# The expert loop of a mixture-of-experts stage: ScalarE's order written out by hand, and other PSUM banks for the last expert's products

## The chip, the cores and the metric

The kernel runs on one core of one Trainium2 chip. The metric is the device time of one execution in microseconds; lower is better. The core has a TensorE (PE) for matrix products and transposes, a VectorE (DVE), a ScalarE (ACT), a GpSimd (POOL), and a SyncE (SP) that here issues the loads. PE writes its products into PSUM, which this stage divides into eight banks of 512 fp32 numbers per partition; everything else lives in SBUF.

## The reference, cut to what matters

The program computes two transformer blocks in a row on 1024 positions of width 1024, in fp32. The change touches only the mixture of experts that ends block one: 32 experts of inner width 512, two per token.

```python
D_MODEL = 1024; SEQ = 1024; N_EXPERTS = 32; TOP_K = 2; D_EXPERT = 512
def hier_moe(xn, w_route_group, b_route_group, w_route_expert, b_route_expert, w_gate, w_up, w_down):
...
    def expert_block(args):
        xblk, e = args
        hdn = jax.nn.silu(xblk @ w_gate[e]) * (xblk @ w_up[e])
        return hdn @ w_down[e]
...
def first_block(...):
...
        h = h + mixed @ w_out[l]
        h = h + hier_moe(rms_norm(h, norm2_gain[l]), ...)
    return rms_norm(h, final_norm_gain)
```

`second_block` (attention, two convolution mixers and a feed-forward part) follows on that result.

## The kernel before, in words

**One expert.** Each expert has 96 slots for tokens. Its six weight tiles of 1 MB (`mw`: two of gate, two of up, two of down) are loaded on SP's queue into a ring of 17 buffers (L996), so that a load is issued when the tile 17 places ahead of it has been used. An fp32 product is made of three fast ones (`mm3`, L38 to L40): each operand is split into a rounded part (`hi`, a ScalarE copy) and the rest (`lo`, a VectorE subtraction that follows it), and PE adds hi times lo, lo times hi and hi times hi. `split` (L1158 on ScalarE, L1163 on VectorE) does it for half a weight tile at a time, into a ring of four pairs `mhi`, `mlo`. An expert e goes through:

- `gather`: GpSimd fetches the 96 rows of its tokens into `xg`;
- `xT`: PE turns them round with eight transposes into PSUM (`mtr`, L1173), ScalarE evicts them as `xhi` (two instructions, L1176) and as `xf` (L1179), VectorE makes `xlo`;
- `up`: four chunks each of gate (`pg`) and up (`pu`): eight splits, 42 fast matmuls and two in plain fp32 (from `xf`, L1192, each drawn as two), then `silu` on ScalarE (`hd<-pg`, L1198) and the multiply with `pu` on VectorE (`hd<-hd,pu`, L1199);
- `down`: four transposes of `hd` (L1205), the split of the result (`hhi`, L1210; `hlo`, L1211), and 24 matmuls over four chunks of down's weights into `py`; then ScalarE copies `py` to SBUF (`ye<-py`, L1223) and GpSimd scatters it to memory (L1224). For the last expert VectorE copies one half (L1220) and ScalarE the other (L1221), and its `hhi` and `hlo` lie in buffers named `xhi` and `xlo`.

**PSUM.** `pg`, `pu` and `mtr` have two buffers of one bank each. `py` has a single buffer of two banks, so that all eight banks are taken: the next expert's first product into `py` has to wait until `ye<-py` has read it.

**Order.** The program writes up(e), xT(e+1), gather(e+2), down(e-1) for each e, and a scheduler puts the instructions of each engine's queue in order, by its own estimates and by a few priorities (`high_priority` on silu, the multiply, and the eviction of `hd`'s transposes). Engines take their queues in the order so fixed, which is the same in every execution. Behind the last expert come loads of the scattered rows, a sum and a normalization, and then block two; while the last expert runs, ScalarE and VectorE already split some weights of block two (`wthi`, `wtlo`, L1393 and L1394).

Of the kernel before, what the change touches and what calls it, by code (L numbers as in the profile page):

```python
# [12 lines left out]
F32 = mybir.dt.float32  # L13
F32R = mybir.dt.float32r
# [6 lines left out]
P = 128  # L21
# [998 lines left out]
def moe(tc, K, a, xn, lg, w12, yd, wst, s_m, then):  # L1020
# [119 lines left out]

    ps = xctx.enter_context(tc.tile_pool(name="mps", bufs=2, space=PSUM))

    def expert(xg, idx_g, idx_s, get, nye, last=False, behind=None):

        st = {}

        def gather():
            return nc.gpsimd.indirect_dma_start(out=xg, out_offset=None, in_=xn,  # L1148
                                                in_offset=bass.IndirectOffsetOnAxis(ap=idx_g, axis=0),
                                                bounds_check=S - 1, oob_is_err=False)  # L1150

        def split(w, c):
            if c % 2 == 0:
                st[w] = get()
            n = 512 if w != "d" and c == 3 else 1024
            src = st[w][:, (c % 2) * 1024:(c % 2) * 1024 + n]
            hi, lo = (t[:, 0:n] for t in spl.tiles([([P, 1024], "mhi"), ([P, 1024], "mlo")], F32R, len(spl.slots)))
            nc.scalar.activation(hi, src, AF.Copy)  # L1158
            with ExitStack() as held:
                if behind:  # L1160
                    held.enter_context(tc.issue_after(behind.ins))
# [4 lines left out]
        def xT():  # L1166
            hi = act.tile([P, 7, SLOTS], F32R, name="xhi")
            lo = act.tile([P, 7, SLOTS], F32R, name="xlo")
            xf = act.tile([P, SLOTS], F32, name="xf")
            for q in range(2):  # L1170
                p = ps.tile([P, 4, SLOTS], F32, name="mtr")
                for k in range(4):
                    nc.tensor.transpose(p[:, k, :], xg[:, 4 * q + k::8], K.ident[:SLOTS, :SLOTS])  # L1173
                n = 4 - q
                h = hi[:, 4 * q:4 * q + n, :]
                nc.scalar.activation(h, p[:, 0:n], AF.Copy)  # L1176
                V.tensor_sub(lo[:, 4 * q:4 * q + n, :], p[:, 0:n], h.bitcast(F32))  # L1177
                if q:
                    nc.scalar.activation(xf, p[:, 3], AF.Copy)  # L1179
            st["x"] = hi, lo, xf  # L1180

        def up():
            pg = ps.tile([SLOTS, 512], F32, name="pg")
            pu = ps.tile([SLOTS, 512], F32, name="pu")
            xhi, xlo, xf = st["x"]
            for c in range(4):
                for w, o in (("g", pg), ("u", pu)):
                    hi, lo = split(w, c)
                    for j in range(2):
                        k = 2 * c + j  # L1190
                        if k == 7:
                            nc.tensor.matmul(o, xf, st[w][:, 1536:2048], start=False, stop=True)  # L1192
                            continue
                        mm3(nc, o, xhi[:, k, :], xlo[:, k, :], hi[:, j * 512:(j + 1) * 512],
                            lo[:, j * 512:(j + 1) * 512], k == 0, False)
            hd = act.tile([SLOTS, 512], F32, name="hd", bufs=1)
            with tc.high_priority(offset=MPRI):
                nc.scalar.activation(hd, pg, AF.Silu)  # L1198
                V.tensor_mul(hd, hd, pu)  # L1199
            st["h"] = hd  # L1200

        def down():
            p = ps.tile([P, 4, SLOTS], F32, name="mtr")
            for k in range(4):
                nc.tensor.transpose(p[:, k, :], st["h"][:, k::4], K.ident[:SLOTS, :SLOTS])  # L1205

            hhi, hlo = (act.tile([P, 7, SLOTS], F32R, name="x" + n)[:, 0:4] if last else
                        act.tile([P, 4, SLOTS], F32R, name="h" + n, bufs=1) for n in ("hi", "lo"))
            with tc.high_priority(offset=MPRI):
                nc.scalar.activation(hhi, p, AF.Copy)  # L1210
                V.tensor_sub(hlo, p, hhi.bitcast(F32))  # L1211
            py = ps.tile([SLOTS, 1024], F32, name="py", bufs=1)
            for k in range(4):
                hi, lo = split("d", k)
                for c in range(2):
                    mm3(nc, py[:, c * 512:(c + 1) * 512], hhi[:, k, :], hlo[:, k, :],
                        hi[:, c * 512:(c + 1) * 512], lo[:, c * 512:(c + 1) * 512], k == 0, k == 3)
            y = act.tile([SLOTS, D], F32, name="ye", bufs=nye)
            if last:
                V.tensor_copy(y[:, 0:512], py[:, 0:512])  # L1220
                nc.scalar.activation(y[:, 512:], py[:, 512:], AF.Copy)  # L1221
            else:
                nc.scalar.activation(y, py, AF.Copy)  # L1223
            return nc.gpsimd.indirect_dma_start(  # L1224
                out=yd, out_offset=bass.IndirectOffsetOnAxis(ap=idx_s, axis=0), in_=y, in_offset=None,
                bounds_check=2 * S - 1, oob_is_err=False)

        return gather, xT, up, down
# [5 lines left out]
    E = [expert(xgs[e % NX], gidx[:SLOTS, e:e + 1], sidx[:SLOTS, e:e + 1], wst.get, 2, e + 1 == NE, None if e else known)  # L1234
         for e in range(NE)]
    scat = []
    for e in range(NX):
        g = E[e][0]()
# [23 lines left out]
    with tc.If(over > 0):  # L1262
# [23 lines left out]
        with tc.For_i(0, NE, 1) as e:  # L1286
            n = nc.values_load(nb[0:1, bass.ds(e, 1)], min_val=0, max_val=MORE + 1)
            with tc.For_i(1, n, 1) as b:
                V.tensor_copy(si, sof[:, bass.ds(e * MORE + b - 1, 1)])
                V.tensor_copy(gi, gof[:, bass.ds(e * MORE + b - 1, 1)])  # L1290

                def dyn(w, i):
                    return [P, 2048], lambda t: nc.sync.dma_start(
                        t, a[WN[w]][bass.ds(e, 1), :, i * 2048:(i + 1) * 2048].rearrange("o p f -> (o p) f"))
                ws = Stream(raw, [dyn(w, i) for w2 in ("gu", "d") for i in range(2) for w in w2], 5, "mw")
                for f in expert(xg, gi[:SLOTS], si[:SLOTS], ws.get, 1):
                    f()
        ctx.close()


# [1067 lines left out]
```

## Time and profile before

| | us |
|---|---|
| median of 3 runs (lowest to highest) | 2686.21 (2682.15 to 2687.73) |
| the profiled execution, its own time | 2681.36 |
| its span, first to last instruction | 2679.6 |
| first multiply `hd<-hd,pu` (expert 0) to the last (expert 31), starts | 831.24 to 1421.69 |

The rows shown further down are of the one profiled execution. Times count from the first instruction; "x2" at a row's end means two instructions drawn together; an idle time in brackets lies ahead of the instruction, with what ended it behind the arrow. The granted clock (PEclk) is PE's clock as a share of full speed, 1.00 being 2.4 GHz. The multiply L1199 occurs once per expert and so serves as a milestone: the stretch between two of them is one expert's turn.

### The profile page before, as it was taken

What the parts mean: (1) busy time and instruction counts of PE and PEld (TensorE: products, weight loads), DVE (VectorE), ACT (ScalarE), POOL (GpSimd) and SP (SyncE); (2) the same over time, 40 slices, a digit from 0 to 9 for tenths busy, and PEclk for the clock granted to TensorE, in tenths of its full rate; (3) what the DMA queues carried; (4) which work ended last, traced back from release to release, by engine and by line L of the source; (5) the groups of instructions that cost most, each with busy time, mean ns of one, the idle gap of its engine ahead of it and who ended that gap; (6) DMA issues with size and microseconds to landing.
All of it is one profiled execution on the core that took longest, in us unless ns stands there. A gap on an engine that the chain in (4) does not pass through costs nothing.

```text
span 2679.6 us, 42090 instructions
## 1 busy us (share of the span) xinstructions
PE 2519.2 (94%) x15498; PEld 1961.9 (73%) x15499; DVE 1872.9 (70%) x3258; ACT 1385.2 (52%) x2503; POOL 615.6 (23%) x1144
## 2 busy tenths in 40 slices
PE   7999999998988999999995999999999999999998
PEld 5777777776776676666664888777787788888786
DVE  5565767677347878877776664677558898777757
ACT  6443444444226777767675432456545445455444
POOL 1344566665212111111102212212010110000001
PEclk9999999998998999999997999999999999999999
DMA  5533112113478999989866211002124663224935
GB/s 185 168 111 101 51 38 66 29 45 140 158 282 300 371 382 366 362 334 347 331 237 232 86 48 32 24 1 62 58 81 136 225 215 119 83 79 148 341 121 181
DMA packets 170820, 447.11 MB, mean 167 GB/s; under 512 B 42928, under 2 KB 82224, under 8 KB 146032
## 3 DMA queue, kind: packets, MB, share of 16 engines
q1 hardware_dynamic: 150848, 381.17, 40.4%
q0 software_dynamic: 19760, 63.20, 6.5%
q8 instruction: 124, 2.03, 0.3%
q14 instruction: 88, 0.72, 0.1%
HBM read 382.43 MB, written 70.25 MB: 169 GB/s over the span
## 4 chain that ended last, share of the span: by engine, by line
PE 57%; issue 23%; DVE 8%; POOL 6%; DMA 3%; ACT 2%; SPq 0%; POOLq 0%; DVEq 0%; ACTq 0%
PE pa L1993 8%; PE pj L38 6%; PE pj L39 6%; PE pj L40 6%; PE pd L1993 4%; PE pe L1993 2%; PE po L38 2%; PE po L39 2%; PE po L40 2%; POOL xg L1148 2%; PE pe L2219 2%; PE O L1845 2%; PE px L2219 2%; PE T L1835 1%; POOL yd L1224 1%
## 5 line engine op out<-in xcount | busy, mean ns | idle before, releaser
L1163 DVE TENSOR_TENSOR mlo<-mw,mhi 128x1024 fp32r<-128x1024 f32 (+1 forms) x384 | 427.0, 1133 | 133.7 <-ACT mhi L1158 131.6
L1158 ACT ACTIVATE mhi<-mw 128x1024 fp32r<-128x1024 f32 (+1 forms) x384 | 375.6, 986 | 161.4 <-PE py L40 51.5
L38 PE MATMUL py<-mhi,hlo 128*96 128x512 f32 x248 | 106.1, 428 | 20.2 <-ACT ye L1223 15.1
L1224 POOL DMA_INDIRECT yd<-ye,sidx x32 | 35.3, 1103 | 360.6 <-ACT ye L1223 352.8
L2047 DVE SCALAR_TENSOR_TENSOR y<-c,pc,y 128x1023 f32<-128x1023 f32 x88 | 111.9, 1278 | 5.6 <-ACT y L2045 5.5
L38 PE MATMUL pj<-whi,xlo 128*128 128x512 f32 x256 | 106.3, 415 | 1.1 <-DVE gh L476 1.1
L39 PE MATMUL pj<-wlo,xhi 128*128 128x512 f32 x256 | 103.4, 404 | 0.0
L40 PE MATMUL pj<-whi,xhi 128*128 128x512 f32 x256 | 103.3, 403 | 0.0
L40 PE MATMUL py<-mhi,hhi 128*96 128x512 f32 x248 | 99.5, 401 | 0.0
L39 PE MATMUL py<-mlo,hhi 128*96 128x512 f32 x248 | 99.4, 401 | 0.0
L38 PE MATMUL pu<-mhi,xlo 128*96 128x512 f32 x224 | 96.6, 431 | 0.0
L38 PE MATMUL pj<-xhi,wclo 128*128 128x512 f32 x224 | 91.3, 407 | 4.2 <-ACT pj L1471 4.2
L39 PE MATMUL pu<-mlo,xhi 128*96 128x512 f32 x224 | 95.0, 424 | 0.0
L662 POOL TENSOR_TENSOR Xt<-Tm,Xi 128x15 f32<-128x15 f32 (+7 forms) x240 | 73.9, 308 | 76.3 <-DVE Tm L655 61.6
L38 PE MATMUL pj<-xhi,wlo 128*128 128x512 f32 x224 | 89.3, 403 | 1.9 <-ACT xhi L278 1.1
L39 PE MATMUL pj<-xlo,whi 128*128 128x512 f32 x224 | 90.5, 404 | 0.3 <-DVE xlo L279 0.3
L40 PE MATMUL pj<-xhi,wchi 128*128 128x512 f32 x224 | 90.5, 404 | 0.0
L38 PE MATMUL pg<-mhi,xlo 128*96 128x512 f32 x224 | 89.8, 401 | 0.5 <-DVE xlo L1177 0.5
L39 PE MATMUL pj<-xlo,wchi 128*128 128x512 f32 x224 | 90.3, 403 | 0.0
L40 PE MATMUL pj<-xhi,whi 128*128 128x512 f32 x224 | 90.2, 403 | 0.0
L1148 POOL DMA_INDIRECT xg<-xnd,gidx x32 | 44.5, 1390 | 195.3 <-PE mtr L1173 186.8
L39 PE MATMUL pg<-mlo,xhi 128*96 128x512 f32 x224 | 89.2, 398 | 0.0
(729 smaller groups left out, 7603.6 us busy)
## 6 DMA issues: line engine op xcount, KB each, us to landing
mw<-w_down SPq DMA_DIRECT2D x64, 1024.0 KB, 10.1
mw<-w_up SPq DMA_DIRECT2D x63, 1024.0 KB, 7.5
mw<-w_gate SPq DMA_DIRECT2D x62, 1024.0 KB, 9.5
wf<-ffn_up SPq DMA_DIRECT2D x44, 512.0 KB, 3.4
hr<-hdn SPq DMA_DIRECT2D x77, 256.0 KB, 5.0
w<-w_rwkv SPq DMA_DIRECT2D x28, 512.0 KB, 4.8
tq<-ffn_down SPq DMA_DIRECT2D x44, 256.0 KB, 3.6
td<-tq POOLq DMA_DIRECT2D x22, 512.0 KB, 3.6
```

Source lines behind the costliest of these rows:

```text
L38: nc.tensor.matmul(out, ll, rh, start=first, stop=False)
L39: nc.tensor.matmul(out, lh, rl, start=False, stop=False)
L40: return nc.tensor.matmul(out, lh, rh, start=False, stop=last)
L662: G.tensor_tensor(y, Tm[:, j + 1:16, j:j + 1].to_broadcast([P, n, m]), X[:, j:j + 1, 0:m].to_broadcast([P, n, m]), op=OP.mult)
L1148: return nc.gpsimd.indirect_dma_start(out=xg, out_offset=None, in_=xn, in_offset=bass.IndirectOffsetOnAxis(ap=idx_g, axis=0), bounds_check ...
L1158: nc.scalar.activation(hi, src, AF.Copy)
L1163: V.tensor_sub(lo, src, hi.bitcast(F32))
L1224: return nc.gpsimd.indirect_dma_start(out=yd, out_offset=bass.IndirectOffsetOnAxis(ap=idx_s, axis=0), in_=y, in_offset=None, bounds_check= ...
L1845: nc.tensor.matmul(o[64 * x:64 * x + 64], vt[:, k, hd * 64:(hd + 1) * 64], ts[x][:, j], start=(k == 0), stop=(k == qb))
L1993: nc.tensor.matmul(p, l, r[:, k], start=first and k == 0 and i == 0, stop=k == 3 and i == 2, skip_group_check=True)
L2047: V.scalar_tensor_tensor(y[:, n:], c[:, 0:S - n], tap(2 - n), y[:, n:], op0=OP.mult, op1=OP.add)
L2219: nc.tensor.matmul(bank[i], l[:, s], r, start=first and k == 0 and n == 0, stop=k == HB - 1 and n == 2, skip_group_check=True)
```

## The change

The nested function `expert` becomes a class `Expert` with the same instructions, cut into smaller methods. Four things differ in what is built:

1. The loop no longer writes whole stages one behind the other. It writes, for expert e: gate chunk 0, up chunk 0, the eviction `xf` of e, gate chunk 1, the copy and scatter of expert e-2, up chunk 1, `hT` (the transposes of `hd`) of e-1, chunks 2 and 3, down chunks 0 to 2 of e-1, silu of e, down chunk 3 of e-1, then `xT` of e+1 and `gather` of e+2.
2. From expert 1's silu on, every ScalarE instruction of the experts is issued behind the one that was written ahead of it (`chain`): an order on the same queue, with no semaphore. VectorE, PE and GpSimd stay the scheduler's.
3. The last expert's down products go into two buffers of `pg` and `pu` instead of `py`, and its two copies read these.
4. Behind the loop, the copy and scatter of expert 30 are written between down chunks 1 and 2 of expert 31.

```diff
+        def act(self, *args, **kw):
+            with ExitStack() as held:
+                if chained[0] and chain:
+                    held.enter_context(tc.issue_after(chain[-1].ins))
+                ins = nc.scalar.activation(*args, **kw)
+            if chained[0]:
+                chain.append(ins)
...
+        def down(self, k):
+            if k == 0:
+                if self.last:
+                    self.y = [ps.tile([SLOTS, 512], F32, name=n) for n in ("pg", "pu")]
+                else:
+                    py = ps.tile([SLOTS, 1024], F32, name="py", bufs=1)
+                    self.py, self.y = py, [py[:, c * 512:(c + 1) * 512] for c in range(2)]
...
+            if self.last:
+                V.tensor_copy(y[:, 0:512], self.y[0])
+                self.act(y[:, 512:], self.y[1], AF.Copy)
...
-    E[0][1]()
-    for e in range(NE):
-        E[e][2]()
+    for e, x in enumerate(E):
+        y = E[e - 1] if e else None
+        x.product("g", 0)
+        x.product("u", 0)
+        if e:
+            x.whole()
+        x.product("g", 1)
+        if e > 1:
+            scat.append(E[e - 2].store())
+        x.product("u", 1)
+        if y:
+            y.hT()
+        for c in range(2, 4):
+            for w in "gu":
+                x.product(w, c)
+        for k in range(3) if y else ():
+            y.down(k)
+        x.silu()
+        if y:
+            chained[0] = True
+            y.down(3)
         if e + 1 < NE:
-            E[e + 1][1]()
+            E[e + 1].xT()
         if NX <= e + 2 < NE:
-            E[e + 2][0]()
-        if e:
-            scat.append(E[e - 1][3]())
-    scat.append(E[NE - 1][3]())
+            E[e + 2].gather()
+    x.hT()
+    x.down(0)
+    x.down(1)
+    scat.append(y.store())
+    x.down(2)
+    x.down(3)
+    scat.append(x.store())
```

**ScalarE, one expert in the second half of the loop.** In ScalarE's queue of the kernel before, from the silu of expert 18 to that of expert 19 (here `ye` is the copy of expert 16, and `hhi` belongs to expert 18):

```order
L1198 ACTIVATE hd<-pg 96x512
L1158 ACTIVATE mhi<-mw 128x1024
L1223 ACTIVATE ye<-py 96x1024
L1158 ACTIVATE mhi<-mw 128x1024 x6
L1176 ACTIVATE xhi<-mtr 128x384
L1176 ACTIVATE xhi<-mtr 128x288
L1158 ACTIVATE mhi<-mw 128x512 x2
L1179 ACTIVATE xf<-mtr 128x96
L1158 ACTIVATE mhi<-mw 128x1024 x2
L1210 ACTIVATE hhi<-mtr 128x384
L1158 ACTIVATE mhi<-mw 128x1024
L1198 ACTIVATE hd<-pg 96x512
```

In the changed kernel, from the silu of expert 18 on (here `ye` is the copy of expert 17, and `hhi` belongs to expert 18):

```order
L1158 ACTIVATE hd<-pg 96x512
L1158 ACTIVATE mhi<-mw 128x1024
L1158 ACTIVATE xhi<-mtr 128x384
L1158 ACTIVATE xhi<-mtr 128x288
L1158 ACTIVATE mhi<-mw 128x1024 x2
L1158 ACTIVATE xf<-mtr 128x96
L1158 ACTIVATE mhi<-mw 128x1024
L1158 ACTIVATE ye<-py 96x1024
L1158 ACTIVATE mhi<-mw 128x1024
L1158 ACTIVATE hhi<-mtr 128x384
L1158 ACTIVATE mhi<-mw 128x1024 x2
L1158 ACTIVATE mhi<-mw 128x512 x2
```

The copy of `py` has moved from behind the silu of the next expert but one to the middle of the expert that follows its own, and `hhi` from the end of the expert to its middle. Before, the order that the changed kernel has throughout stands for experts 1 to 11; from expert 12 on `ye` slips back, and from expert 15's silu to expert 30's it mostly stands one or two places behind a silu, as in the first fence.

**ScalarE, from the last silu on.** Before (`xhi` is the eviction of expert 31's transposed `hd`, the `ye` that of expert 30, the `mhi` are splits of down's weights):

```order
L1158 ACTIVATE mhi<-mw 128x1024 x2
L1393 ACTIVATE wthi<-wt_15437,pc_67 128x452
L1158 ACTIVATE mhi<-mw 128x1024
L1393 ACTIVATE wthi<-wt_15441,pc_67 128x452
L1393 ACTIVATE wthi<-wt_15445,pc_67 128x452
L1158 ACTIVATE mhi<-mw 128x1024
L1393 ACTIVATE wthi<-wt_15449,pc_67 128x452
L1210 ACTIVATE xhi<-mtr 128x384
L1393 ACTIVATE wthi<-wt_15453,pc_67 128x452
L1393 ACTIVATE wthi<-wt_15457,pc_67 128x452
L1223 ACTIVATE ye<-py 96x1024
L1158 ACTIVATE mhi<-mw 128x1024
```

After:

```order
L1158 ACTIVATE hd<-pg 96x512
L1158 ACTIVATE mhi<-mw 128x1024
L1158 ACTIVATE xhi<-mtr 128x384
L1158 ACTIVATE mhi<-mw 128x1024 x2
L1452 ACTIVATE wthi<-wt_15438,pc_67 128x452
L1452 ACTIVATE wthi<-wt_15442,pc_67 128x452
L1158 ACTIVATE ye<-py 96x1024
L1158 ACTIVATE mhi<-mw 128x1024 x2
```

The eviction `xhi` has moved from behind three splits of expert 31's down weights to ahead of all of them, and four of the `wthi` from ahead of `ye` to behind the last split.

**PE, the last expert's down products.** Before (`mtr<-ident,hd` are the transposes of expert 31's `hd`; the products with `hhi` are those of expert 30, the ones with `xhi`, `xlo` those of expert 31):

```order
L1205 MATMUL mtr<-ident,hd 128x96 x4
L39 MATMUL py<-mlo,hhi 96x512
L40 MATMUL py<-mhi,hhi 96x512
L38 MATMUL py<-mhi,hlo 96x512
L39 MATMUL py<-mlo,hhi 96x512
L40 MATMUL py<-mhi,hhi 96x512
L38 MATMUL py<-mhi,xlo 96x512
L39 MATMUL py<-mlo,xhi 96x512
L40 MATMUL py<-mhi,xhi 96x512
```

After (the products into `pg` and `pu` are those of expert 31):

```order
L1221 MATMUL mtr<-ident,hd 128x96 x4
L39 MATMUL py<-mlo,hhi 96x512
L40 MATMUL py<-mhi,hhi 96x512
L38 MATMUL py<-mhi,hlo 96x512
L39 MATMUL py<-mlo,hhi 96x512
L40 MATMUL py<-mhi,hhi 96x512
L38 MATMUL pg<-mhi,xlo 96x512
L38 MATMUL pu<-mhi,xlo 96x512
L39 MATMUL pg<-mlo,xhi 96x512
L40 MATMUL pg<-mhi,xhi 96x512
L39 MATMUL pu<-mlo,xhi 96x512
L40 MATMUL pu<-mhi,xhi 96x512
```

On PE the transposes `xT` move too: before, those of expert e+2 stand in the turn of expert e up to expert 12, and those of e+1 from then on; after, those of e+1 do throughout. No other instruction of an expert's turn on PE, VectorE or GpSimd is added or taken away, and SP's loads keep their order.

The products of expert 31 stand where they stood in the second pair of fences, but go into two buffers that no copy of expert 30 has to free, and chunk by chunk the two halves alternate.

## Rows read from the trace of the kernel before

**Rows 1.** The page, busy time: us, share of the span, instructions.

```profile
PE 2519.2 (94%) x15498; PEld 1961.9 (73%) x15499; DVE 1872.9 (70%) x3258; ACT 1385.2 (52%) x2503; POOL 615.6 (23%) x1144
```

**Rows 2.** VectorE in order of time, gate times up: start us, us, engine, line, operation.

```profile
862.35 0.68 DVE L1199 TENSOR_TENSOR hd<-hd,pu 96x512 f32<-96x512 f32 x1
...
1063.65 0.68 DVE L1199 TENSOR_TENSOR hd<-hd,pu 96x512 f32<-96x512 f32 x1
1081.09 0.68 DVE L1199 TENSOR_TENSOR hd<-hd,pu 96x512 f32<-96x512 f32 x1
...
1117.70 0.68 DVE L1199 TENSOR_TENSOR hd<-hd,pu 96x512 f32<-96x512 f32 x1
...
1421.69 0.68 DVE L1199 TENSOR_TENSOR hd<-hd,pu 96x512 f32<-96x512 f32 x1
```

**Rows 3.** Stretches: us, busy us of PE, PEld, DVE, ACT, POOL; clock, DMA share, GB/s.

```profile
862.35:1117.70 255.35, 254.82 (x1138) 176.19 (x1136) 208.50 (x226) 196.92 (x253) 30.24 (x26) 1.00 0.96 373
1117.70:1421.69 303.99, 282.27 (x1225) 192.04 (x1226) 228.18 (x239) 214.71 (x269) 36.35 (x28) 0.98 0.83 312
...
1081.09:1099.40 18.31, 18.31 (x86) 12.75 (x85) 15.27 (x18) 13.50 (x19) 1.81 (x1) 1.00 0.97 367
```

**Rows 4.** TensorE's waits, 1117.70 to 1421.69: us in total, times, longest us.

```profile
PE py L38 <- ACT ye L1223: 15.1, 10, 1.6
PE py L38 <- DVE hlo L1211: 5.2, 2, 2.6
PE mtr L1205 <- DVE hd L1199: 2.0, 1, 2.0
```

**Rows 5.** ScalarE in order of time: two copies of `py`; brackets hold the wait before.

```profile
867.64 1.02 ACT L1223 ACTIVATE ye<-py 96x1024 f32<-96x1024 f32 x1 [0.50 <-PE py L40]
...
1117.66 1.01 ACT L1223 ACTIVATE ye<-py 96x1024 f32<-96x1024 f32 x1
```

**Rows 6.** TensorE in order of time: products behind a wait, and one soon after.

```profile
1118.72 0.47 PE L38 MATMUL py<-mhi,hlo 128*96 128x512 f32 x1 [1.56 <-ACT ye L1223]
1119.03 0.39 PE L39 MATMUL py<-mlo,hhi 128*96 128x512 f32 x1
1119.26 0.39 PE L40 MATMUL py<-mhi,hhi 128*96 128x512 f32 x1
...
1139.83 0.44 PE L38 MATMUL py<-mhi,hlo 128*96 128x512 f32 x1 [2.58 <-DVE hlo L1211]
...
1141.36 0.63 PE L40 MATMUL py<-mhi,hhi 128*96 128x512 f32 x1
```

**Rows 7.** Weight tiles `mw`, issue to landing: first 862.35 to 990, then 990 to 1117.70.

```profile
DMA to landing us min/median/max: 7.6/10.9/12.0
...
DMA to landing us min/median/max: 7.5/9.9/11.7
```

**Rows 8.** TensorE in order of time, from the last expert's multiply on.

```profile
1425.40 0.61 PE L1205 MATMUL mtr<-ident,hd 96*128 96x96 f32 x4
...
1430.26 0.47 PE L38 MATMUL py<-mhi,xlo 128*96 128x512 f32 x1 [3.09 <-ACT ye L1223]
```

**Rows 9.** ScalarE and VectorE in the same stretch, in order of time.

```profile
1427.70 0.47 ACT L1210 ACTIVATE xhi<-mtr 128x384 fp32r<-128x384 f32 x1
...
1429.50 0.55 DVE L1211 TENSOR_TENSOR xlo<-mtr,xhi 128x384 fp32r<-128x384 f32 x1
...
1432.33 1.28 DVE L1394 SCALAR_TENSOR_TENSOR wtlo<-wt,pc,wthi 128x452 fp32r<-128x452 f32 x2
...
1437.63 0.69 DVE L1220 COPY ye<-py 96x512 f32<-96x512 f32 x1 [4.03 <-PE py L40]
...
1438.36 0.59 ACT L1221 ACTIVATE ye<-py 96x512 f32<-96x512 f32 x1 [6.08 <-DVE ye L1220]
```

**Rows 10.** Splits of weights: ns shortest, median, longest; first and last start.

```profile
L1158 ACT ACTIVATE mhi<-mw x384: 617/1059/1066, 798.3 to 1430.1; 128x1024 fp32r<-128x1024 f32 x160, 128x512 fp32r<-128x512 f32 x32
L1163 DVE TENSOR_TENSOR mlo<-mw,mhi x384: 675/1224/1265, 807.4 to 1431.2; 128x1024 fp32r<-128x1024 f32 x160, 128x512 fp32r<-128x512 f32 x32
```

More of the change, by code (lines that the diff above doesn't have):

```diff
@@ L1180, in xT @@
[L1180 to L1196, printed above, removed]
+            self.p7 = p[:, 3]
@@ new lines, in whole, with product @@
+        def whole(self):
+            self.xf = act.tile([P, SLOTS], F32, name="xf")
+            self.act(self.xf, self.p7, AF.Copy)
+        def product(self, w, c):
+            if w == "g" and c == 0:
+                self.o = {"g": ps.tile([SLOTS, 512], F32, name="pg"), "u": ps.tile([SLOTS, 512], F32, name="pu")}
+            o, (xhi, xlo) = self.o[w], self.x
+            hi, lo = self.split(w, c)
+            for j in range(2):
+                k = 2 * c + j
+                if k == 7:
+                    nc.tensor.matmul(o, self.xf, self.w[w][:, 1536:2048], start=False, stop=True)
+                    continue
+                mm3(nc, o, xhi[:, k, :], xlo[:, k, :], hi[:, j * 512:(j + 1) * 512],
+                    lo[:, j * 512:(j + 1) * 512], k == 0, False)
@@ L1197, in up, with silu, hT @@
+        def silu(self):
+            self.h = act.tile([SLOTS, 512], F32, name="hd", bufs=1)
             with tc.high_priority(offset=MPRI):
[L1198 to L1202, printed above, removed]
+                self.act(self.h, self.o["g"], AF.Silu)
+                V.tensor_mul(self.h, self.h, self.o["u"])
+        def hT(self):
             p = ps.tile([P, 4, SLOTS], F32, name="mtr")
             for k in range(4):
-                nc.tensor.transpose(p[:, k, :], st["h"][:, k::4], K.ident[:SLOTS, :SLOTS])
-            hhi, hlo = (act.tile([P, 7, SLOTS], F32R, name="x" + n)[:, 0:4] if last else
-                        act.tile([P, 4, SLOTS], F32R, name="h" + n, bufs=1) for n in ("hi", "lo"))
+                nc.tensor.transpose(p[:, k, :], self.h[:, k::4], K.ident[:SLOTS, :SLOTS])
+            hhi, hlo = self.hs = [act.tile([P, 7, SLOTS], F32R, name="x" + n)[:, 0:4] if self.last else
+                                  act.tile([P, 4, SLOTS], F32R, name="h" + n, bufs=1) for n in ("hi", "lo")]
@@ L1209, in down @@
             with tc.high_priority(offset=MPRI):
-                nc.scalar.activation(hhi, p, AF.Copy)
+                self.act(hhi, p, AF.Copy)
                 V.tensor_sub(hlo, p, hhi.bitcast(F32))
-            py = ps.tile([SLOTS, 1024], F32, name="py", bufs=1)
-            for k in range(4):
[L1214 to L1226, printed above, removed]
@@ L1228, in expert @@
-        return gather, xT, up, down
+        def down(self, k):
[5 more added lines that the diff above has]
+                    self.py, self.y = py, [py[:, c * 512:(c + 1) * 512] for c in range(2)]
+            hi, lo = self.split("d", k)
+            for c in range(2):
+                mm3(nc, self.y[c], self.hs[0][:, k, :], self.hs[1][:, k, :],
+                    hi[:, c * 512:(c + 1) * 512], lo[:, c * 512:(c + 1) * 512], k == 0, k == 3)
@@ new lines, in store @@
+        def store(self):
+            y = act.tile([SLOTS, D], F32, name="ye", bufs=self.nye)
+            if self.last:
+                V.tensor_copy(y[:, 0:512], self.y[0])
+                self.act(y[:, 512:], self.y[1], AF.Copy)
+            else:
+                self.act(y, self.py, AF.Copy)
+            return nc.gpsimd.indirect_dma_start(
+                out=yd, out_offset=bass.IndirectOffsetOnAxis(ap=self.idx_s, axis=0), in_=y, in_offset=None,
+                bounds_check=2 * S - 1, oob_is_err=False)
@@ L1230, in moe, with all @@
+        def all(self):
+            self.gather()
+            self.xT()
+            self.whole()
+            for c in range(4):
+                for w in "gu":
+                    self.product(w, c)
+            self.silu()
+            self.hT()
+            for k in range(4):
+                self.down(k)
+            self.store()
     NX = 2
@@ L1233, in moe @@
         nc.gpsimd.memset(x, 0.0)
[L1234 removed]
+    E = [Expert(xgs[e % NX], gidx[:SLOTS, e:e + 1], sidx[:SLOTS, e:e + 1], wst.get, 2, e + 1 == NE, None if e else known)
          for e in range(NE)]
@@ L1295, in moe @@
                 ws = Stream(raw, [dyn(w, i) for w2 in ("gu", "d") for i in range(2) for w in w2], 5, "mw")
-                for f in expert(xg, gi[:SLOTS], si[:SLOTS], ws.get, 1):
-                    f()
+                Expert(xg, gi[:SLOTS], si[:SLOTS], ws.get, 1).all()
         ctx.close()
```

43 lines of the change are left out of this document (23 added, 20 removed).

## The prediction

> **What bounds the kernel now.** I read the page first: PE is busy for 94% of the span [rows 1], so the time goes where PE idles or runs slowly, and elsewhere only if PE is made to wait. The change touches the experts alone, so next I took VectorE in order of time and used the multiply that closes each expert's `up` as a milestone [rows 2]. From expert 2 (862.35) to expert 16 (1117.70) there are 14 turns in 255.35 us; from there to expert 31 (1421.69) there are 15 in 303.99 us, that is 20.27 us each. In the first stretch 13 of the 14 turns take 18.30 us (the last two together 36.61) and one takes 17.44 (1063.65 to 1081.09). That one has no `xT`: before, the scheduler lets the transposes run two experts ahead until there and one ahead from there. So eight transposes are worth 0.86 us of PE.
>
> The stretches say why the two halves differ [rows 3]. In the first PE is busy for 254.82 of 255.35 us at clock 1.00, with ScalarE at 196.92 and VectorE at 208.50: 18.30 us is PE's own work, and nobody else's pace. In the second PE is busy for 282.27 of 303.99 us, at a mean clock of 0.98. The table of PE's waits there names 22.3 us [rows 4]: ten times 1.5 us for `ye`, the copy that empties `py`; twice 2.6 us for `hlo`; once 2.0 us for `hd`. The same table of the first stretch is empty. The two copies show the mechanism [rows 5]. A regular one starts at 867.64, 5.3 us after the multiply at 862.35, as soon as PE has ended the products it copies (ScalarE waited 0.50 us for them). A late one starts at 1117.66, with no wait ahead of it: ScalarE's queue simply had it behind the silu and one more split. PE had run out of gate's and up's products and stood for 1.56 us until `py` was free [rows 6]. In the order of ScalarE's queue this is the `ye` that slips from the middle of an expert to behind a silu, and `hhi` to the end of the turn; the 2.58 us for `hlo` is the latter. Behind it the product at 1141.36 lasts 0.63 us where others take 0.39 (and follow each other by 0.23), so the idle time also costs some clock.
>
> **The change, part by part.** I add it up against the profiled execution's own 2681.36 us, which is 4.85 us under the median of the runs; I assume the changed kernel's median lies as far above its own profile, so the 4.85 comes on at the end.
>
> First, the order. The changed queue of ScalarE has, for experts 1 to 31, row for row the order that the old one has in the stretch without waits; VectorE's and PE's rows between two multiplies are those of that stretch as well. No wait is added: the order is one on ScalarE's own queue, without a semaphore. What stands behind each ScalarE instruction is then what stood behind it in 14 measured turns, and there no wait of PE came of it. So I take 18.30 us for a turn. The last one, `up` of expert 31, has no transposes left: 17.44. From expert 2 to expert 31 that is 29 × 18.30 − 0.86 = 529.84 us, against 1421.69 − 862.35 = 559.34 now: **−29.50 us**. Ahead of expert 2's multiply PE has eight transposes fewer, since `xT` runs one expert ahead and no longer two, and PE has no gap there to lose them in: **−0.86 us**. What this takes is nothing new in cost: the classes, the interleaved code and the earlier scatter are the same instructions. The copy on ScalarE and the scatter on GpSimd (busy for 30 to 36 us in either stretch [rows 3]) come earlier, with room.
>
> A faster loop asks the DMA queues for more. The weights now come at 312 GB/s in the second half and would have to come at the first half's 373, at a DMA share of 0.96 [rows 3]. That this can be kept up for 29 turns instead of 14 shows in the time from issue to landing: its median is 10.9 us in the first half of that stretch and 9.9 in the second, so no queue builds up [rows 7]; the ring of 17 tiles covers 17/6 of a turn, some 52 us. Cost taken: none.
>
> Second, the end. Now the last multiply starts at 1421.69 and the last copy ends at 1438.36 + 0.59, 17.26 us later [rows 9]. The transposes of `hd` end at 1426.0 [rows 8], but ScalarE evicts them only at 1427.70, behind three splits, and PE then stands 3.09 us for `ye` of expert 30, the `py` wait once more [rows 8]. With `pg` and `pu` that wait is gone. I replayed the new order with the old durations: transposes done at +4.3 us after the multiply, `hhi` 0.47, `hlo` done at about +5.3 [rows 8, 9]; then VectorE has four `mlo` at some 1.15 us between starts, six `wtlo` at 0.64 and the copy itself of 0.69 [rows 9, 10], 4.6 + 3.8 + 0.7, and waits about 0.6 us for the split that ScalarE issues behind `ye`: +15.0. That is **−2.3 us**. Bounds: if PE alone set the end, the transposes at +3.7 us (0.4), the 29 products behind them (five of expert 30, 24 of expert 31) at 0.23 each [rows 6, 8] and the copy of 0.7 would end at +11.5, that is −5.8; if VectorE's `wtlo` or a wait pushes the copy out again, 0. The value lies nearer to VectorE's queue because `COPY` now stands behind four `wtlo`. Everything behind the scatter starts from its end and moves along unchanged.
>
> Sum: −29.50 − 0.86 − 2.3 = −32.7; 2681.36 − 32.7 = 2648.7; plus 4.85 gives **2653.5 us**. With both ends of the last term it is 2650.0 to 2655.8; some turns with a short wait (a dozen of 0.5 us) and the runs' own spread of some 3 us either way take it to 2646 and 2663.
>
> **The rivals.** *The weights fall behind.* For it: a DMA share of 0.96 to 0.97 leaves little. A turn moves 373 GB/s × 18.24 us = 6.80 MB; at the 367 GB/s of the turn from 1081.09 [rows 3], if that were the most to be had, a turn would take 18.53 us and the loop lose 29 × 0.23 = 7 us: 2660. Against it are the steady landings [rows 7]. The Trainium skill ("DMA: Bandwidth & Descriptors", section "Where 436 GB/s comes from") has the memory's share of one core, about 358 GB/s, bind such transfers; that would be an estimated 19.0 us a turn and about 2673. The trace disagrees: 373 GB/s as a mean over 255 us.
>
> *The pace doesn't hold; the change does half of what it says.* Only ScalarE's order is fixed; VectorE's and PE's are the scheduler's, and the old waits for `hd` and `hlo` (7.2 us) are not for the copy. If half of the second stretch's loss stays: 2653.5 + 16 = 2670. Against it: in the built order all turns read alike on the three engines.
>
> *Slower.* ScalarE's queue now can't slip anything forward. If in each turn `ye` or `hhi` reaches the head before PE has made its input, the splits behind it come late, `mlo` after them, and PE waits for a weight, every turn alike. At the 1.56 us of a late turn [rows 6] that costs 29 × 1.56 = 45 us against 32.7 won: 2653.5 + 45 = 2698, slower than before. It decides from 32.7/29 = 1.13 us a turn. For it speaks that `ye` does wait at the head, by 0.50 us [rows 5]. Against it: this is in the regular stretch, where PE lost 0.53 of 255 us in all. The Trainium skill ("PSUM — Partial Sum Buffer", section "Engine vs sequencer instructions") calls ScalarE's queue strictly first in, first out, so that such a wait does hold up all behind it; the trace agrees, in the late `ye` that had no wait of its own.
>
> **How the numbers follow.** Forecast 2653.5 (2646 to 2663): 0.82. Weights behind, 2660: 0.05. Half, 2670: 0.06. Slower, 2698: 0.04. A milder form of that, 0.9 to 1.2 us a turn, which eats the gain: 0.03. The range 2645 to 2667 holds the first two nearly whole, and a part of the third. A measurement of this kernel can tell about 0.2% (5.4 us) from no change; by that, faster 0.93, same 0.03, slower 0.04.
>
> **What would show it.** Right: multiplies 18.30 us apart from expert 2 to 30 and 17.4 before the last; no PE wait for `ye` or `hlo`; every copy some 5.3 us behind a multiply; DMA share 0.96 over the whole loop, with landings still near 10 us; clock 1.00 there; the last copy ends some 15 us after the last multiply, and the rest of the program shifted as a block. Wrong: turns over 18.5 us with ScalarE waiting on `mw`'s DMA (weights), or PE waiting for `mhi` or `mlo` behind a `ye` or `hhi` that waits (slower), or new waits for `ye` (half); and any change of block two beyond a shift, which I hold to be untouched.

## The result, and the profile after

The changed kernel takes 2656.59 us (median of 4 runs, 2653.85 to 2657.79) against 2686.97 us of the kernel before on the same chip: a ratio of 0.9888, interval 0.9871 to 0.9906. A second set of runs gave 2655.74 us against 2685.81, 0.9889 (0.9869 to 0.9909). So 30 us, 1.1%, are won. The forecast was 2653.5 us.

The page of the changed kernel, its span and PE's busy time, answers to [rows 1]:

```profile
span 2656.1 us, 42102 instructions
...
PE 2518.7 (95%) x15498; PEld 1964.3 (74%) x15499; DVE 1866.4 (70%) x3258; ACT 1383.0 (52%) x2503; POOL 600.4 (23%) x1144
```

VectorE's multiplies in order of time, for [rows 2]; the columns are start, duration, engine, line, operation:

```profile
864.99 0.68 DVE L1216 TENSOR_TENSOR hd<-hd,pu 96x512 f32<-96x512 f32 x1
...
883.29 0.67 DVE L1216 TENSOR_TENSOR hd<-hd,pu 96x512 f32<-96x512 f32 x1
...
1121.03 0.68 DVE L1216 TENSOR_TENSOR hd<-hd,pu 96x512 f32<-96x512 f32 x1
...
1139.35 0.67 DVE L1216 TENSOR_TENSOR hd<-hd,pu 96x512 f32<-96x512 f32 x1
...
1377.36 0.68 DVE L1216 TENSOR_TENSOR hd<-hd,pu 96x512 f32<-96x512 f32 x1
...
1394.82 0.68 DVE L1216 TENSOR_TENSOR hd<-hd,pu 96x512 f32<-96x512 f32 x1
```

Every turn from expert 2 to expert 30 takes 18.26 to 18.32 us and the last one 17.46; from 864.99 to 1394.82 are 529.83 us. That stretch, and its first half, in the view of the stretches, for [rows 3]:

```profile
864.99:1394.82 529.83, 529.83 (x2371) 366.95 (x2370) 430.16 (x465) 410.04 (x523) 55.67 (x55) 1.00 0.94 359
864.99:1129.90 264.91, 264.91 (x1190) 184.04 (x1189) 216.00 (x235) 206.12 (x264) 31.01 (x29) 1.00 0.97 373
```

PE is busy through all of it, at clock 1.00. (The whole stretch has 359 GB/s only because the last weights are loaded before it ends: up to 1300 it is 374, at a DMA share of 0.98.) The table of PE's waits over these 529.83 us is empty; that is what has become of [rows 4]. A copy of `py`, for [rows 5], now has its place in every turn; ScalarE comes to it a little ahead of PE and waits 0.3 us, 28 times in the loop:

```profile
1126.08 1.02 ACT L1158 ACTIVATE ye<-py 96x1024 f32<-96x1024 f32 x1 [0.27 <-PE py L40]
```

The end, for [rows 8] and [rows 9], in order of time on PE, on VectorE and ScalarE, and on PE again:

```profile
1398.52 0.60 PE L1221 MATMUL mtr<-ident,hd 96*128 96x96 f32 x4
...
1400.65 0.48 PE L38 MATMUL pg<-mhi,xlo 128*96 128x512 f32 x1 [0.37 <-ACT mhi L1158]
...
1401.91 0.48 PE L39 MATMUL pg<-mlo,xhi 128*96 128x512 f32 x1 [0.56 <-DVE mlo L1178]
...
1409.23 0.68 DVE L1244 COPY ye<-pg 96x512 f32<-96x512 f32 x1
...
1408.75 0.57 ACT L1158 ACTIVATE ye<-pu 96x512 f32<-96x512 f32 x1
...
1429.68 2.69 PE L293 MATMUL tr<-diag,y 128*128 128x128 f32 x11 [21.29 <-DMA y<-yd]
```

PE no longer stands 3.09 us for `ye` of expert 30 but 0.37 and twice 0.56 us for splits, and no product behind them is slow. The last copy ends at 1409.91, 15.09 us behind the last multiply, where it was 17.26. PE takes up block one's last normalization 34.86 us behind the multiply, where it was 35.90: about half of the 2.2 us is lost again between the copy and the loads that follow the scatter.

### The profile page after: what moved, and what is told of

The parts are those of the page before. It is cut to its first block, busy times and chain, and to the rows that moved or that the text cites. A ratio compares the mean times of both kernels' runs of the same rounds, so it can differ in the third digit from the quotient of the medians.

```text
span 2656.1 us, 42102 instructions
## 1 busy us (share of the span) xinstructions
PE 2518.7 (95%) x15498; PEld 1964.3 (74%) x15499; DVE 1866.4 (70%) x3258; ACT 1383.0 (52%) x2503; POOL 600.4 (23%) x1144
## 4 chain that ended last, share of the span: by engine, by line
PE 78%; DVE 9%; issue 4%; DMA 4%; ACT 3%; POOL 3%; SPq 0%; DVEq 0%; POOLq 0%; ACTq 0%
PE pa L2052 6%; PE pj L38 6%; PE pj L39 6%; PE pj L40 6%; PE pd L2052 3%; PE pu L38 2%; PE pu L39 2%; PE pu L40 2%; PE py L40 2%; PE py L38 2%; PE py L39 2%; PE px L2278 2%; PE pe L2278 2%; PE pg L38 2%; PE pg L40 2%
## 5 line engine op out<-in xcount | busy, mean ns | idle before, releaser
L39 PE MATMUL pj<-wlo,xhi 128*128 128x512 f32 x256 | 103.1, 403 | 0.0
L39 PE MATMUL pu<-mlo,xhi 128*96 128x512 f32 x228 | 102.2, 448 | 0.0
L39 PE MATMUL py<-mlo,hhi 128*96 128x512 f32 x248 | 97.3, 393 | 0.0
L39 PE MATMUL pg<-mlo,xhi 128*96 128x512 f32 x228 | 90.6, 397 | 1.1 <-DVE mlo L1178 1.1
L39 PE MATMUL pj<-xlo,whi 128*128 128x512 f32 x224 | 90.6, 405 | 0.3 <-DVE xlo L279 0.3
L40 PE MATMUL pg<-mhi,xhi 128*96 128x512 f32 x228 | 90.5, 397 | 0.0
L39 PE MATMUL pj<-xlo,wchi 128*128 128x512 f32 x224 | 90.3, 403 | 0.0
```

The costliest lines, as they stand in the source:

```text
L39: nc.tensor.matmul(out, lh, rl, start=False, stop=False)
L40: return nc.tensor.matmul(out, lh, rh, start=False, stop=last)
```

## The experiments

The theory: in the second half of the loop ScalarE's queue had the copy of `py`, and twice `hhi`, so late that PE ran dry; fixed in the place that it had in the first half, they cost nothing, and PE's own 18.3 us a turn are what remains. Each run lists the loop, from the multiply of expert 2 to that of expert 31 (29 turns), as read from its trace; the kernel before has 559.34 us there and the changed one 529.83.

**e1 and e2: the copy late in every turn.** The edit of e1 takes the copy from its place among the first chunks and puts it behind the silu; e2 puts it behind the split that follows.

```diff
-        if e > 1:
-            scat.append(E[e - 2].store())
...
         x.silu()
+        if e > 1:
+            scat.append(E[e - 2].store())      (e1)
         if y:
             chained[0] = True
             y.down(3)
+        if e > 1:
+            scat.append(E[e - 2].store())      (e2)
```

> The changed kernel with one edit: the copy of py is put directly behind the silu of the next expert but one, in every turn, as the kernel before has it in its turns from expert 15 on (there mostly one row later still). All else, the chain too, stays. My theory (the place of ye in ScalarE's queue is what PE waited for): ye then starts some 0.5 us after silu's start and ends 1.5 us after it, while PE runs out of gate's and up's products about 0.9 us after silu's start; PE waits about 0.6 us for ye in each of some 30 turns, the loop from expert 2 to 31 takes 529.8 + 18 = 548 us, the whole some 18 us over the changed kernel, about 2675. Rival (the waits came of the order as a whole, of hhi and the transposes too, and with these in place a late copy is covered): loop 530 us, time as the changed kernel's, 2657.

> As the run before, with the copy of py one split of weights later still, the place it mostly has in the second half of the kernel before. My theory: another 0.95 us on each turn, a PE wait for ye of some 1.5 us in about 30 turns, loop 529.8 + 45 = 575 us, the whole about 2702, slower than the kernel before. If the clock falls behind these waits, more. Rival (order as a whole): loop 530 us, 2657.

Measured: e1 2681.1 us, loop 554.17 us, turns of 19.14; e2 2698.2 us, loop 581.44 us, turns of 20.08 (one run each; the kernel before, run beside them, has 2686.37). PE's waits in the loop, e1 first (total, times, longest), and one of e2's turns on ScalarE and PE:

```profile
PE py L38 <- ACT ye L1158: 17.7, 29, 0.6
```

```profile
PE py L38 <- ACT ye L1158: 45.2, 29, 1.6
```

```profile
1121.54 0.57 ACT L1158 ACTIVATE hd<-pg 96x512 f32<-96x512 f32 x1
1122.02 1.04 ACT L1158 ACTIVATE mhi<-mw 128x1024 fp32r<-128x1024 f32 x1
1122.96 1.00 ACT L1158 ACTIVATE ye<-py 96x1024 f32<-96x1024 f32 x1
...
1124.02 0.47 PE L38 MATMUL py<-mhi,hlo 128*96 128x512 f32 x1 [1.56 <-ACT ye L1158]
```

The copy starts behind silu and one split, with no wait of its own, and PE's wait of 1.56 us is that of [rows 6], now 29 times over. Over the whole loop of e2 the stretch reads:

```profile
861.97:1443.41 581.44, 536.28 (x2370) 364.44 (x2370) 442.96 (x466) 412.35 (x524) 65.14 (x55) 1.00 0.86 327
```

One split more (0.95 us between two starts) costs 0.94 us a turn. So the mechanism is shown, in size too, and it is strong enough to turn 30 us won into 12 us lost. What a late copy costs was put too low, though: e1 lost 24.3 us with 17.7 us of named waits, e2 51.6 with 45.2. In both some 0.23 us a turn come on top of the wait, at a clock of 1.00. PE's rows show where it goes, first those of the changed kernel without the wait, then those of e2 with it:

```profile
1119.48 1.02 PE L1207 MATMUL pu<-mw,xf 128*96 128x512 f32 x2
1119.93 0.79 PE L38 MATMUL py<-mhi,hlo 128*96 128x512 f32 x1
1120.57 0.39 PE L39 MATMUL py<-mlo,hhi 128*96 128x512 f32 x1
```

```profile
1121.44 1.02 PE L1207 MATMUL pu<-mw,xf 128*96 128x512 f32 x2
...
1124.33 0.39 PE L39 MATMUL py<-mlo,hhi 128*96 128x512 f32 x1
```

In these rows a product without a wait starts while the one ahead of it still runs; behind a wait it starts when that one has long ended. From the start of the plain products to that of L39 it is 1.09 us without the wait and 2.89 with it, 1.80 more for a named wait of 1.56: the 0.24 us are the overlap that is lost.

**e3: without the chain.** One line, `chained[0] = True`, is set to `False`, so that nothing is chained.

> The changed kernel without the chain: the code in its new order, but ScalarE's queue left to the scheduler. The queue as built has no steady pattern: the copy of py stands 5 to 9 rows behind a silu in most turns, directly or one row behind it in three (experts 15 to 17). My theory: what counts is only that ye stands early enough, so only those three turns wait for it (0.5 to 1.5 us each), and hhi stands late in none; loop 530 to 537 us, time 2657 to 2664. Rival (it is the fixed order that brings the gain, and any drift costs): loop 545 to 560 us, time 2672 to 2687.

Measured: 2703.04 us, ratio to before 1.0062 (1.0043 to 1.0082); loop 573.7 us. It is slower than the kernel before, and my expectation was wrong. Up to expert 16 its turns take 17.2 to 18.5 us; then up to 24. PE's waits in the loop:

```profile
PE pg L38 <- DVE xlo L1191: 23.1, 12, 2.1
PE py L38 <- ACT ye L1158: 4.7, 3, 1.6
```

The copy is late three times only, as its place in the queue said. But the scheduler, left alone, also puts the evictions `xhi` of the next expert's rows right ahead of their use, so that PE starts an expert with a wait for `xlo`, twelve times, of 2.0 us in eleven of them and 0.62 us in one. Behind eight of the eleven it also runs slowly: such turns take 21.7 us and more, at a mean granted clock of 0.92 to 0.93, where those behind the other three take 20.6 at 1.00. The first of the eight:

```profile
1131.47 0.47 PE L38 MATMUL pg<-mhi,xlo 128*96 128x512 f32 x1 [2.05 <-DVE xlo L1191]
...
1132.43 0.63 PE L38 MATMUL pg<-mhi,xlo 128*96 128x512 f32 x1
```

What I had overlooked is that the written order changes what the scheduler makes of every step, not of the copy alone. The gain needs the chain: the new order of the code without it loses 17 us.

**e4 and e6: the last expert's banks.** e4 gives the kernel before the two banks and nothing else; e6 takes them from the changed kernel (its edit is shown).

```diff
-                if self.last:
-                    self.y = [ps.tile([SLOTS, 512], F32, name=n) for n in ("pg", "pu")]
-                else:
-                    py = ps.tile([SLOTS, 1024], F32, name="py", bufs=1)
-                    self.py, self.y = py, [py[:, c * 512:(c + 1) * 512] for c in range(2)]
+                py = ps.tile([SLOTS, 1024], F32, name="py", bufs=1)
+                self.py, self.y = py, [py[:, c * 512:(c + 1) * 512] for c in range(2)]
```

> The kernel before with only the last expert's down products put into the banks of pg and pu; the loop's order is the old one. My theory: the 3.09 us wait for ye of expert 30 goes, but hhi is still evicted behind three splits and VectorE still has its wtlo ahead of the copy, so from the last multiply to the last copy's end 17.3 us become 15.5 to 16.5; the whole 1 to 2 us faster than before, 2685, within what can be told. Rival: the tail is hidden behind the weights' splits anyway, 0.

> The changed kernel with the last expert's down products back in py; order and chain stay. PE must wait for ye of expert 30, which ScalarE issues behind two splits and two wthi. From the last multiply, which was 15.09 us ahead of the last copy's end in the changed kernel: ye ends at about +8.8 us, PE then has 24 products, +14.4, and the copies: +15.9 to +17.0 (the last splits and wtlo run meanwhile). So the banks are worth 1 to 2 us of the 30. Rival (VectorE's wtlo set the end, not PE): 15.1, banks worth nothing.

Measured: e4 2681.91 us, ratio 0.9988 (0.9978 to 0.9997); from the last multiply to the last copy's end 16.12 us, and its loop, 557.76 us, is 1.58 us shorter, nearly all in the last turn. e6 2651.83 us (one run); the same stretch 17.48 us, loop 529.83. PE's first product of expert 31's down in e4, then in e6:

```profile
1431.85 0.74 PE L38 MATMUL pg<-mhi,xlo 128*96 128x512 f32 x1 [2.94 <-DVE xlo L1211]
```

```profile
1402.43 0.74 PE L38 MATMUL py<-mhi,xlo 128*96 128x512 f32 x1 [3.34 <-DVE wtlo L1450]
```

In e4 the wait for `ye` has only changed its name: PE waits 2.94 us for `xlo`, since `hhi` is still evicted behind three splits. In e6 it is `py` again (the row names what VectorE did last, but `ye<-py` had ended 0.06 us before), 3.34 us long. So the whole 2.17 us take banks and order together: 15.09 us with both, 16.12 with the banks alone, 17.48 with the order alone, 17.26 with none. But less of it reaches the work behind: PE takes up the last normalization 35.90 us behind the last multiply before, 35.94 in e6, 34.73 in e4 and 34.86 in the changed kernel (one profile each), so that there the banks alone are worth the 1 us and the order adds nothing. Either is below what the whole time can show (e6's one run even lies under the changed kernel's median, by differences outside the experts that are told of below).

**e5: how much the DMA queues had left.** One of the three fast products is left out in the experts, so that PE needs less than VectorE; the result is not the reference's.

```diff
+def mm2(nc, out, lh, ll, rh, rl, first, last):
+    nc.tensor.matmul(out, ll, rh, start=first, stop=False)
+    return nc.tensor.matmul(out, lh, rh, start=False, stop=last)
...
-                mm3(nc, o, xhi[:, k, :], ...
+                mm2(nc, o, xhi[:, k, :], ...
```

> The changed kernel with one of the three fast products left out everywhere in the experts (rounded inputs times the weights' rest): PE has 22 products fewer a turn, some 5 us, so that PE no longer sets the turn, and the weights must come faster if anything else lets them. It tells how much the DMA queues had left at 18.3 us a turn. PE's turn would be 13.2 us, VectorE is busy for some 14.8 us a turn. Theory of the prediction (the DMA has a little room, a share of 0.96 at 373 GB/s): it becomes the bound near a share of 1.00, 385 GB/s or 17.6 us a turn, with ScalarE waiting for weights. Rival of the prediction (373 is already the most): 18.2 us a turn, no gain. Third: the DMA has much room, and the turn comes near VectorE's 15 to 15.5 us at 440 GB/s.

Measured: 2602.95 us, loop 490.75 us. Its first seven turns take 14.45 us each; then most take 17.3 to 18.9, some 17.9 in the mean. The stretch behind them, and ScalarE's largest sum of waits there:

```profile
982.00:1343.39 361.39, 304.18 (x1217) 178.38 (x1216) 301.67 (x326) 274.25 (x365) 39.87 (x38) 0.99 1.00 383
```

```profile
ACT mhi L1164 <- DMA mw<-w_down: 37.1, 29, 2.3
```

The table has nearly as much, 36.3 us, for `xhi` waiting for PE's transposes (of which e8 tells), so the pace of 17.9 us isn't shown to be the weights' alone. But the queues are full: a DMA share of 1.00 and, in the list of DMA issues, 23 to 25 us from a weight's issue to its landing, where the changed kernel has 11.1 in the median. So 383 GB/s, and 389 in the stretch ahead, are the most that this loop got, against 373 that a turn of 18.3 us needs: the changed kernel has a margin of 3%. The rival "the weights fall behind" was close but not there. The Trainium skill's lower figure, about 358 GB/s ("DMA: Bandwidth & Descriptors", section "Where 436 GB/s comes from"), is exceeded here by 7%.

**e7 and e8: a fixed ScalarE queue against a free PE queue.** Two further edits of the changed kernel. e7 was meant as an improvement: the last eighth of the inner width, which PE did in plain fp32 from `xf`, is split and multiplied like the rest. e8 evicts `hd`'s transposes four splits later.

```diff
...
-                if k == 7:
-                    nc.tensor.matmul(o, self.xf, self.w[w][:, 1536:2048], start=False, stop=True)
-                    continue
                 mm3(nc, o, xhi[:, k, :], xlo[:, k, :], hi[:, j * 512:(j + 1) * 512],
-                    lo[:, j * 512:(j + 1) * 512], k == 0, False)
+                    lo[:, j * 512:(j + 1) * 512], k == 0, k == 7)      (e7)
...
-        if y:
-            y.hT()
         for c in range(2, 4):
             for w in "gu":
                 x.product(w, c)
+        if y:
+            y.hT()                                                    (e8)
```

> The changed kernel with the last eighth of the inner width, so far one plain fp32 product each for gate and up, done in three fast products as the other seven eighths are; xf goes, ScalarE splits 1024 in place of 512 in two splits a turn (+0.85 us less 0.23) and VectorE likewise (+1.1 us). If PE's own work sets the turn, as I hold, a plain product (0.86 us from its start to the next one's, less) becomes three of 0.23, so that a turn takes 18.30 - 2 x 0.17 = 17.96 us and the loop 521 us: about 10 us faster than the changed kernel, 2647. Rival 1: the DMA can't give the 380 GB/s: turn at 18.3, no gain. Rival 2: VectorE (some 15.9 us busy of 18) makes PE wait: slower, 18.5 us or more a turn.

> The changed kernel with the eviction of hd's transposes put four splits later in ScalarE's queue, behind the third and fourth chunk of gate and up; ye stays early. In the kernel before, two turns waited 2.6 us for hlo because hhi stood at the very end of the turn. Theory (only a place behind the need costs): hhi runs some 13.5 us after the multiply, hlo a microsecond later, the first product that needs it at some 17.2 us: no wait, loop 530 us, 2657. Rival (every row that hhi slips costs PE): waits for hlo in each turn, loop over 545 us.

Measured: e7 2672.97 us, ratio to before 0.9963 (0.9949 to 0.9977), loop 552.57 us: 13 of its first 14 turns take 17.94 to 18.00 us as worked out, the other 17.13, and then they take 18.9 to 21.6. e8 2693.53 us (one run), loop 569.83: the same picture, 18.3 up to expert 13, then mostly 20.3 and more. Neither theory nor rival: the waits are ScalarE's. In e8, ScalarE's waits in the loop that are longest in sum, one of them in order of time, and PE's transposes there:

```profile
ACT xhi L1158 <- PE mtr L1187: 99.0, 19, 5.4
```

```profile
1145.07 1.05 ACT L1158 ACTIVATE mhi<-mw 128x1024 fp32r<-128x1024 f32 x1
1151.53 0.86 ACT L1158 ACTIVATE xhi<-mtr 128x384 fp32r<-128x384 f32 x2 [5.41 <-PE mtr L1187]
1152.28 1.99 ACT L1158 ACTIVATE mhi<-mw 128x1024 fp32r<-128x1024 f32 x2
...
1150.91 1.02 PE L1187 MATMUL mtr<-ident,xg 96*128 96x96 f32 x8
1152.66 0.72 PE L1221 MATMUL mtr<-ident,hd 96*128 96x96 f32 x4 [0.73 <-DVE xlo L1191]
...
1154.33 0.47 PE L38 MATMUL pu<-mhi,xlo 128*96 128x512 f32 x1 [0.48 <-ACT mhi L1158]
```

ScalarE has `xhi` next and may not go on to the splits behind it. PE's queue, which the chain doesn't hold, has the eight transposes behind all of the previous expert's down products in e8 from expert 13 on, at 1150.91. So ScalarE stands for 5.41 us; `xlo`, which frees the PSUM buffer for the transposes of `hd`, and the splits behind come late, and PE waits in its turn, 0.73 us for the one and 0.48 for the other. ScalarE does so 19 times in the loop. Three of e8's turns and four of e7's take another 1.4 to 1.5 us: behind the same two waits the granted clock falls there. This is the mechanism of the rival "slower" of the prediction, with the input of `xhi` late instead of that of `ye` or `hhi`. The Trainium skill's strictly ordered queue ("PSUM — Partial Sum Buffer", section "Engine vs sequencer instructions") is borne out: nothing on ScalarE passes the waiting eviction.

**e9 and e10: PE's transposes fixed too.** Both edits again, with the transposes written as steps of their own: those of `hd` ahead of gate's and up's third chunk, those of the next expert's rows ahead of the fourth, and PE's products of these chunks issued behind them. Shown is the main part of e9; e10 leaves the eviction of `hd`'s transposes ahead of the third chunk.

```diff
+        with ExitStack() as held:
+            if y:
+                held.enter_context(tc.issue_after(y.hturn().ins))
+            x.product("g", 2)
+            x.product("u", 2)
+        with ExitStack() as held:
+            if e + 1 < NE:
+                held.enter_context(tc.issue_after(E[e + 1].turn().ins))
+            x.product("g", 3)
+            x.product("u", 3)
+            if y:
+                y.hT(True)
+            for k in range(3) if y else ():
+                y.down(k)
...
```

> Run e8 (hhi four splits later) with one thing more: the order of PE's transposes is fixed too. Those of hd stand ahead of the third chunk, those of the next expert's rows ahead of the fourth, and PE's products of these chunks are issued behind them; ScalarE's queue is that of e8. In e8, PE's queue had the next expert's eight transposes at the very end of the turn from expert 13 on, ScalarE stood at their eviction (99 us in all, up to 5.4 us at a time) with the splits behind it, and the loop took 569.8 us. Theory (the loss is PE's free order against ScalarE's fixed one, not the place of hhi): turns of 18.3 us throughout, loop 530 us, no wait of ScalarE for the transposes over 1 us, time about 2655. Rival (hhi that late costs PE by itself): turns over 19 us from expert 13 on, loop over 550.

> Run e7 (last eighth in three fast products) with the order of PE's transposes fixed in the same way. In e7 the first 12 turns took 17.99 us, as worked out; from then on PE's queue as built had the transposes late, ScalarE stood at their eviction (63.6 us), and turns took 18.9 to 21.6. Theory: turns of 17.99 us throughout, loop 29 x 17.99 - 0.86 = 520.9 us against 529.8 of the changed kernel, whole 9 us faster than that, about 2647. Rival (weights: 6.80 MB in 17.99 us are 378 GB/s, and the run with two products showed 384 at most; the ring, full at the start, hides a lag of a few per cent only for a while): turns creep up to 18.2 or 18.3 in the second half with ScalarE waiting for weights, 2650 to 2655.

> The changed kernel itself, once more, beside e10 on the same chip: 2653 to 2658 us, ratio to before 0.987 to 0.991; loop from expert 2 to 31 again 529.8 us. What its time differs by from run to run then lies outside that loop.

Measured: e9 2655.49 us (one run), loop 529.58 us, and no wait of PE in it; e8's 40 us were PE's order against ScalarE's, and this place of `hhi` costs nothing. e10 2643.99 us (median of 5), ratio to before 0.9841 (0.9826 to 0.9857), loop 520.69 us, turns of 17.7 to 18.2 (the last 17.1) and 17.95 in the mean. Beside it on the same chip the changed kernel, e11, has 2655.74 us and again a loop of 529.83. So e10 beats both kernels, the changed one by 12 us, of which 9.1 lie in the loop, as worked out. Its two halves, and the weights' time from issue to landing in the first:

```profile
865.52:1129.00 263.48, 263.48 (x1231) 190.28 (x1230) 237.85 (x238) 218.79 (x251) 32.17 (x29) 1.00 1.01 379
1129.00:1386.21 257.21, 257.21 (x1201) 185.81 (x1200) 229.95 (x228) 212.34 (x243) 27.20 (x26) 1.00 0.92 347
```

```profile
DMA to landing us min/median/max: 6.8/8.4/10.4
```

PE is busy throughout, so PE still sets the pace. The first half runs at 379 GB/s, 1% under what e5 got, yet nothing waits for a weight and the landings are short: the DMA queues' limit is near, but not reached.

## Why the prediction was right, point by point

- **The loop, −29.50 us forecast.** 559.34 − 529.83 = 29.51 us. The turn of 18.30 us and the last one without transposes (17.44 forecast, 17.46 measured) were read from the old stretch without waits [rows 2, 3], and no new wait came. That the price was right is no accident of sums: e1 and e2 put a late `ye` back and got the loss back. The smaller part that fell to `hhi` and `hd` before (7.2 us of named waits) was not put back by itself.
- **Ahead of expert 2, −0.86.** The turn of expert 0 is 11.60 us where it was 12.42: −0.82.
- **The end, −2.3.** The last copy's end moved from +17.26 to +15.09: −2.17, at +15.0 as replayed, and in the way replayed: PE's last product ends at 1408.40 and VectorE's copy, behind its `wtlo`, starts at 1409.23. But 1.1 us of it don't reach the program behind: the scatter is issued 0.76 us behind the copy, where it was 0.27, and the loads behind it take up the rest. The step by which everything behind the scatter "moves along unchanged" is off by that.
- **No growth of the DMA queues.** Held: landings of 11.1 us in the median, 14.6 at most, and no wait for a weight. e5 puts the margin at 3%.
- **"In the built order all turns read alike on the three engines"** was not so. ScalarE's and VectorE's do; PE's transposes stand elsewhere from about expert 11 on, one group of eight in place of two of four. In this kernel it cost nothing, which as far as the prediction goes was luck: e7 and e8 show that two small edits let the same group slip a few places further, and the loop lost 23 and 40 us. The argument against the rival "the pace doesn't hold" was this false reading, so that its chance of 0.06 had little ground; and "slower" was judged from the regular stretch alone, where the group had not slipped.
- **The offset, +4.85.** It cancels in the sum: the forecast is the median on record then, 2686.21, less 32.7. With a fourth run that median is 2686.97, and the forecast would have been 2654.3, 2.3 us from the result; 1.1 of these are the scatter's. But profiles can't be compared by their spans: the changed kernel's lies 1.2 us above its median, that of before lay under its own, so spans differ by 23.5 us where medians differ by 30.4. The 7 us between are outside the loop: the first multiply came at 831.24 us in the one profile and at 834.70 in the other, and from PE's take-up of the last normalization to the end it took 1222.0 and 1226.4, with as many instructions on each engine. Over all profiles here the first multiply starts between 828.8 and 836.4, and that last part takes between 1216.8 and 1228.9 us; how much of this is the kernels' and how much differs from run to run isn't shown (the changed kernel's two profiles differ by 0.2 and 1.0 us).

The likeliest case came. Of the rivals, e8 shows the mechanism of "slower", an eviction at the head of ScalarE's queue that waits for PE, and a loss of 40 us where 45 were put. The weights' rival was priced by 367 GB/s as the most to be had; e5 shows 383. "The pace doesn't hold" was not tried by itself.

What stays open: why the queues that the scheduler makes leave their pattern part of the way through the loop in most of these kernels (between expert 6 and 16; in e2 PE's transposes keep it to the end). No trace here shows it, and it was not tried.

## What to carry to other kernels

Where a loop's turns differ although their work is the same, take the regular turn as the price of the irregular ones, and look in the queues for the step that moved; here it predicted a 530 us loop to 0.1 us. A fixed order on one engine can lose more than it gains when an engine that feeds the head of its queue is left free: a step that slips there stalls everything behind its consumer (e7, e8), and ordering the producer too took the loss away (e9, e10). And judge a change inside one stage by that stage's own milestones, since the rest of a long program may differ from profile to profile by a third of the gain.

## What was not expected of the hardware

- A wait costs PE more than its length: 0.22 to 0.23 us a turn beyond the named 0.6 or 1.56 us (e1, e2), the overlap of products that is lost.
- In e2 PE stood idle for 1.56 us in every turn and its clock was 1.00 over all of the loop. Behind waits of 2.58 [rows 6], 2.94 (e4) and 3.34 us (e6), and behind eight of e3's eleven waits of 2.0 us, products of 0.63 us follow instead of 0.39; behind the other three they don't. Nor does it take one long wait: in e8, twelve transposes with a wait of 0.73 us among them and one of 0.48 us behind are followed by products of 0.63 us in three turns, at a granted clock of 0.50 (1.2 GHz), and in others not. Two microseconds of one such turn, with the columns of [rows 3]:

```profile
1194.00:1196.00 2.00, 2.00 (x6) 1.28 (x6) 2.00 (x3) 2.00 (x3) 0.00 (x0) 0.50 0.87 348
```

- The core's DMA queues moved 383 to 389 GB/s at most in the loop, weights and all (e5), and at 379 GB/s with a DMA share of 1.01 nothing waited for a weight (e10).
